# A mixture of experts on one core: experts ordered by token count on the chip, and narrow passes for the small ones

## The chip, the core and the metric

The kernel runs on one core of one Trainium2 chip. The metric is the device time of one execution in microseconds (us), as the median of several runs. A core has an engine for matrix products (TensorE, in the rows PE for its matmuls and PEld for its weight loads), VectorE (DVE), ScalarE (ACT), GpSimd (POOL) and SyncE (SP), which here mostly issues transfers, and 16 DMA engines that move data between the chip's memory (HBM) and the core's own.

## The reference

The program is a decoder of two layers on 256 tokens of 1,024 values. Each layer has a stage of three token mixers with a common projection, which this change leaves alone but for one small matmul, and then a mixture of 16 experts. The router picks, for every token, one of four groups of experts and in it two experts. The reference computes every expert on all tokens and weighs them with the gates, which are zero for the experts not chosen:

```python
gates = jnp.einsum('bske,bsk->bse', jax.nn.one_hot(top_idx, N_EXPERTS, dtype=jnp.float32), top_w).astype(h.dtype)
out = jnp.zeros_like(h)
for e in range(N_EXPERTS):
    a = jax.nn.silu(h @ w_gate[e]) * (h @ w_up[e])
    out = out + (gates[..., e:e + 1] * a) @ w_down[e]
```

`w_gate` and `w_up` of an expert are 1,024 x 512, `w_down` is 512 x 1,024, all float32: 6 MB an expert and 96 MB a layer (1 MB is 1,048,576 bytes here).

## The kernel before, in words

The function `moe()` (from line 833) computes one layer's experts. It needs no expert on all tokens: each expert gets 64 slots (`CAP`), and the tokens that chose it are put into them in the order of their number. The router (lines 880 to 930) leaves, for each token and expert, `rk`, the place of the token among that expert's tokens, counted from 1 and zero where the token did not choose it, and `gate`. `nf` (lines 938 to 940) is the number of 64-slot passes each expert needs.

**Gather.** `group()` (line 1130) compares `rk` with 1 to 64 for four experts at once, which gives a 0/1 matrix `Pm` of 256 tokens by 4 x 64 slots. `gather()` (line 966) multiplies the tokens' values by it on TensorE: for each of 8 blocks of 128 values four matmuls, for two halves of the tokens and for the values split into two fp32r parts `hi` and `lo` (line 974). The results `xg` hold the slots of four experts side by side in 256 columns. A group is gathered when the last expert of the group before has been started.

**One expert, a step of the loop at line 1150.** SP issues its loads: four `w1slot` transfers of 1 MB for gate and up (line 99, in a ring of 11 buffers that all stages share) and three `wd` transfers (two of 0.5 MB at line 1158, with 5 buffers, and one of 1 MB at line 1160, with 2 buffers). SP issues in program order; a transfer whose buffer is still being read holds up all transfers behind it. TensorE then does, mixed with each other by the table `CAB`:

- `up()` (line 1005): 16 matmuls in fp32, each of which the trace records as two, with the expert's 64 slots as the stationary matrix and 512 columns of weights moving. There are two column tiles of 64 (`j`): each holds one half of the expert's hidden values, its gate and up columns in one row of 512;
- `act()` (line 1013): Silu on ACT and the product on DVE, giving `a`; `turn()` (line 1019) transposes it with two matmuls against `ident` (`paT`), and DVE copies it out as `aT`;
- `down()` (line 1027): 8 matmuls `py` of 512 columns, again in two column tiles; ACT and DVE scale them with the gate and split them into `yy`;
- `scatter_tables()` (line 991): the one-hot matrix of the expert transposed (`ppg`, line 994) and its gate column (line 996), as `pT` and `gc`;
- `combine()` (line 1050): 8 matmuls that add the expert's rows to the tokens' places in four accumulators `mo` (line 1060). The last expert of a layer uses its other form, `flat`, with 16 matmuls of 64 rows (line 1055).

The turn, down and combine of an expert lie in the next expert's step (`pend`). `GROUPS = (1, 0, 2, 3)` makes experts 4 to 7 the first group of either layer.

**Overflow.** `extras()` (line 1063) works out, in the first step and on DVE, how many further passes of 64 slots are needed and for which experts. After the loads and the up pass of the step at position 8 (`OVE`), `overflow()` (line 1081) has TensorE, ACT, DVE and SP read that number and branch; for each further pass, `round_()` (line 1101) loads the expert's 6 MB again on SP by a register address (line 1092, four ring buffers `w1ovf`) and does gather, up, down and combine for up to 64 tokens. At most 7 rounds are built into the code, one inside another.

In `trunk()`, lines 243 to 246 write a constant `dup`, two halves of `ident` twice each, which one small matmul at line 516 uses in the mixers' stage.

## Time and profile before

| what | us |
|---|---|
| median of 3 runs | 933.82 (932.88 to 934.24) |
| the profiled execution, its own time | 933.14 |
| the span in its trace | 931.4 |

| engine | busy us in the span | share |
|---|---|---|
| TensorE, matmuls (PE) | 835.0 | 90% |
| VectorE (DVE) | 470.1 | 50% |
| ScalarE (ACT) | 292.0 | 31% |
| GpSimd (POOL) | 77.6 | 8% |

299.10 MB (10^6 bytes) are moved, at a mean of 321 GB/s; the mean granted clock of TensorE is 0.961 of full speed. The experts of layer 0 take the span from about 217 to 475 us, those of layer 1 from about 652 to 925 us. A row of the timeline gives the start in us from the span's start, the duration in us, the engine, the line, the operation, output and inputs by their names, the tile and shape, and how many instructions it stands for; brackets give an idle time before it and what ended it. An fp32 matmul is recorded as two. Matmuls that overlap in the pipeline or in different tiles each show their own time, so the pace is read from starts and not from durations.

### The profile page before, as it was taken

What the parts mean: (1) busy time and instruction counts of PE and PEld (TensorE: products, weight loads), DVE (VectorE), ACT (ScalarE), POOL (GpSimd) and SP (SyncE); (2) the same over time, 40 slices, a digit from 0 to 9 for tenths busy, and PEclk for the clock granted to TensorE, in tenths of its full rate; (3) what the DMA queues carried; (4) which work ended last, traced back from release to release, by engine and by line L of the source; (5) the groups of instructions that cost most, each with busy time, mean ns of one, the idle gap of its engine ahead of it and who ended that gap; (6) DMA issues with size and microseconds to landing.
All of it is one profiled execution on the core that took longest, in us unless ns stands there. A gap on an engine that the chain in (4) does not pass through costs nothing. (4 is left out here: it accounts for less than half of the span.)

```text
span 931.4 us, 12309 instructions
## 1 busy us (share of the span) xinstructions
PE 835.0 (90%) x4646; PEld 474.5 (51%) x4646; DVE 470.1 (50%) x1132; ACT 292.0 (31%) x676; POOL 77.6 (8%) x84
## 2 busy tenths in 40 slices
PE   4799989768999998999979989998999999799995
PEld 3677558744343343343358766786334344234332
DVE  7979989974232132222167998976222213122222
ACT  6255756331111020111155546754111112011110
POOL 2132001310000000000013220111000000000000
PEclk8899899978999999999999989998999999899998
DMA  8958688777999968999955694685889998399981
GB/s 362 419 193 336 274 353 283 274 316 301 370 417 373 395 255 334 420 417 419 419 201 175 246 404 174 238 310 217 301 328 413 376 405 336 141 421 417 418 349 46
DMA packets 47877, 299.10 MB, mean 321 GB/s; under 512 B 5568, under 2 KB 6336, under 8 KB 16320
## 3 DMA queue, kind: packets, MB, share of 16 engines
q1 hardware_dynamic: 46368, 296.05, 80.8%
q10 hardware_dynamic: 1440, 2.16, 0.8%
q8 instruction: 40, 0.66, 0.3%
q14 instruction: 29, 0.24, 0.1%
HBM read 297.13 MB, written 1.05 MB: 320 GB/s over the span
## 5 line engine op out<-in xcount | busy, mean ns | idle before, releaser
L1009 PE MATMUL pgu<-w1slot,xg 128*64 128x512 f32 x1024 | 273.3, 608 | 3.4 <-PEq L1102 3.4
L1009 PEld LDWEIGHTS pgu<-w1slot,xg 128*64 128x64 f32 x1024 | 71.9, 137 | 115.9 <-issue 107.4
L1043 ACT ACTIVATE yy<-py,gc 64x512 fp32r<-64x512 f32 x60 | 41.0, 683 | 227.8 <-PE py L1032 190.1
L1016 DVE TENSOR_TENSOR a<-a,pgu 128x256 f32<-128x256 f32 x33 | 13.9, 421 | 168.2 <-ACT a L1015 168.2
L189 DVE SCALAR_TENSOR_TENSOR adaslot<-adaslot,sb__90 128x1024 f32<-128x1024 f32 x72 | 94.7, 1325 | 0.0
L998 DVE CAST pgT<-ppg 128x256 fp32r<-128x256 f32 x33 | 14.0, 425 | 145.3 <-PE ppg L996 145.3
L344 PE MATMUL pz<-hhi,whl 128*128 128x256 f32 x256 | 73.1, 296 | 10.1 <-ACT hhi L415 10.1
L345 PE MATMUL pz<-hlo,whl 128*128 128x256 f32 x256 | 75.0, 296 | 0.8 <-DVE hlo L416 0.7
L346 PE MATMUL pz<-hhi,whl 128*128 128x256 f32 x256 | 74.3, 296 | 1.0 <-DVE whl L340 1.0
L1015 ACT ACTIVATE a<-pgu 128x256 f32<-128x256 f32 x33 | 12.7, 385 | 191.3 <-PE pgu L1009 191.3
L340 POOL TENSOR_TENSOR whl<-winslot,whl 128x512 fp32r<-128x512 f32 (+1 forms) x24 | 35.2, 1467 | 408.1 <-ACT whl L338 359.1
L1032 PE MATMUL py<-wd,aT 128*64 128x512 f32 x256 | 61.4, 592 | 0.0
L1044 DVE SCALAR_TENSOR_TENSOR yy<-py,gc,yy 64x512 fp32r<-64x512 f32 x60 | 45.0, 750 | 25.7 <-ACT yy L1043 24.7
L1060 PEld LDWEIGHTS mo<-pgT,yy 128*128 128x128 f32 x240 | 32.0, 188 | 49.5 <-DVE yy L1044 47.9
L344 PEld LDWEIGHTS pz<-hhi,whl 128*128 128x128 f32 x256 | 49.5, 198 | 14.2 <-ACT hhi L415 12.9
L345 PEld LDWEIGHTS pz<-hlo,whl 128*128 128x128 f32 x256 | 51.0, 199 | 2.4 <-DVE hlo L416 1.7
L346 PEld LDWEIGHTS pz<-hhi,whl 128*128 128x128 f32 x256 | 50.5, 198 | 2.1 <-DVE whl L340 1.4
L338 ACT CAST whl<-winslot 128x512 fp32r<-128x512 f32 (+1 forms) x72 | 40.3, 577 | 24.2 <-PE pz L346 23.6
L1060 PE MATMUL mo<-pgT,yy 128*128 128x256 f32 x240 | 44.3, 306 | 0.8 <-DVE yy L1044 0.8
L340 DVE TENSOR_TENSOR whl<-winslot,whl 128x512 fp32r<-128x512 f32 (+1 forms) x48 | 35.0, 733 | 10.1 <-ACT whl L338 10.1
L346 PE MATMUL pw<-yhi,whl 128*128 128x256 f32 x128 | 36.5, 291 | 3.5 <-DVE whl L340 3.5
L344 PE MATMUL pw<-yhi,whl 128*128 128x256 f32 x128 | 37.1, 292 | 1.1 <-DVE sge L711 0.7
(490 smaller groups left out, 1390.7 us busy)
## 6 DMA issues: line engine op xcount, KB each, us to landing
w1slot<-w_dram SPq DMA_DIRECT2D x128, 1024.0 KB, 12.2
adaslot<-adaw_dram SPq DMA_DIRECT2D x40, 1024.0 KB, 6.9
wd<-wd_dram SPq DMA_DIRECT2D x32, 1024.0 KB, 7.7
winslot<-win_dram SPq DMA_DIRECT2D x14, 1024.0 KB, 9.9
slot<-adaw_dram SPq DMA_DIRECT2D x8, 1024.0 KB, 18.9
woslot<-wout_dram SPq DMA_DIRECT2D x8, 1024.0 KB, 10.4
slot<-win_dram SPq DMA_DIRECT2D x6, 1024.0 KB, 18.2
cmpslot<-cmpw_dram SPq DMA_DIRECT2D x4, 1024.0 KB, 8.3
```

The lines of the kernel that those rows point to most:

```text
L189: V.scalar_tensor_tensor(wb, wb, 1.0, sb_, op0=OP.mult, op1=OP.mult, accum_out=mv_[:, b:b + 1])
L338: A.copy(hi, wv)
L340: (G if wc[0] % WP[fl[0]] == 0 else V).tensor_tensor(lo, wv, hi.bitcast(F32), op=OP.subtract)
L344: T.matmul(o, a[0], b[0], start=start, stop=False, skip_group_check=True)
L345: T.matmul(o, a[0], b[1], start=False, stop=False, skip_group_check=True)
L346: T.matmul(o, a[1], b[0], start=False, stop=stop, skip_group_check=True)
L998: V.tensor_copy(pT, pp_[:, :S])
L1009: lastu[0] = T.matmul(gu[64 * j:64 * j + 64, :], xg(c)[:, xs:xs + CAP], w1(c, j), start=c == 0, stop=c == 7, skip_group_check=True).ins
L1032: T.matmul(py[64 * hf:64 * hf + 64, :], aT[:, ib, 64 * j:64 * j + 64], wd(fc)[:, 512 * hf:512 * hf + 512], start=fc == 0, stop=fc == 3, sk ...
L1043: ya = A.activation(y[0:64, :], py[r_, :], AF.Copy, scale=gc[r_, :])
L1044: V.scalar_tensor_tensor(y[64:128, :], py[r_, :], gc[r_, :], y[0:64, :].bitcast(F32), op0=OP.mult, op1=OP.subtract)
L1060: T.matmul(mo[db // 2][:, S * (db % 2):S * (db % 2) + S], yy[db // 4][:, P * (db % 4):P * (db % 4) + P], pT, start=False, stop=False, skip ...
```

## The change

All of it lies in `moe()` but for the removal of `dup`. It does six things.

1. **A sort on the chip.** Experts 4 to 7 stay first and keep their 64 slots (`NST`, `ST0`). The other twelve are ordered by their token count, largest first: `sort()` builds a key of 16 times the count plus the expert's number (the four static ones get a key far below), compares all pairs, sums to a rank, and with one-hot products writes `rk`, `gate`, the count and the expert's number in the new order (`rkP`, `gP`, `inP`, `idI`). It runs on DVE, right behind the first group's gather. `extras()` works on the new order and is some instructions longer.
2. **Loads by address.** For positions 4 to 15 SP reads the expert's number from `idI` into a register and loads `w1` and `wd` from there (lines 1258 to 1268 of the changed kernel).
3. **Slots by position.** Positions 0 to 9 have 64 slots; position 4, the largest expert, has 32 more, in a pass of its own with the same weights (`"x"`); positions 10 to 15 have 32. The gathers of the four groups, `XGR`, are 256, 224, 224 and 160 columns wide.
4. **A pass of 32 slots.** `up_few()` uses four column tiles of 32 with 256 moving columns, 32 matmuls in place of 16 of 512; `act()` works on 128 columns of gate and 128 of up on all 128 partitions, and `turn()` is one transpose. `down_few()` has 16 matmuls of 256 columns in place of 8 of 512, and `combine_few()` 16 of 32 rows in four row tiles.
5. **Overflow.** `OVE` goes from 8 to 12, the rounds from 7 to 8. The rounds' weights go through one buffer of 0.5 MB, in twelve pieces, on POOL's queue in place of SP's; SP no longer branches, POOL does (`ENG3` in place of `ENG4`).
6. **Small ones.** `dup` is replaced by two matmuls against halves of `ident`, and the eight last additions into `xT` stand in another order.

The core of the diff:

```diff
+SW = 32
+NST = 4
+ST0 = 4
+HOT = 4
+NBIG = 10
+CAPS = [CAP] * HOT + [CAP + SW] + [CAP] * (NBIG - HOT - 1) + [SW] * (NE - NBIG)
+XGR = (((0, 0, CAP), (1, 64, CAP), (2, 128, CAP), (3, 192, CAP)),
+       ((4, 0, CAP), (5, 64, CAP), (6, 128, CAP), ("x", 192, SW)),
+       ((7, 0, CAP), (8, 64, CAP), (9, 128, CAP), (10, 192, SW)),
+       ((11, 0, SW), (12, 32, SW), (13, 64, SW), (14, 96, SW), (15, 128, SW)))
...
-ENG4 = (mybir.EngineType.PE, mybir.EngineType.Activation, mybir.EngineType.DVE, mybir.EngineType.SP)
-NOVF = 7
-OVE = 8
+ENG3 = (mybir.EngineType.PE, mybir.EngineType.Activation, mybir.EngineType.DVE, mybir.EngineType.Pool)
+NOVF = 8
+OVE = 12
...
+        def sort():
...
+            key = sm_([16], "nf")
+            V.scalar_tensor_tensor(key, idn[:, 1, :], 16.0, kc, op0=OP.mult, op1=OP.add)
...
+            V.tensor_tensor(cmp_, key.unsqueeze(1).to_broadcast([P, 16, 16]), key.unsqueeze(2).to_broadcast([P, 16, 16]), op=OP.is_ge)
+            rank = sm_([16], "gat")
+            V.tensor_reduce(rank, cmp_, axis=AX.X, op=OP.add)
...
+            for src, dst in ((idn, inP), (rk, rkP), (gate, gP)):
+                for r in range(2):
+                    tm = tl("k1", [nd, 16], "tmq")
+                    V.tensor_tensor(tm, oh, src[:, r, :].unsqueeze(1).to_broadcast([P, nd, 16]), op=OP.mult)
+                    V.tensor_reduce(dst[:, r, NST:], tm, axis=AX.X, op=OP.add)
...
+        def up_few(xg, xs, w1, gu=None, cs=range(8)):
+            gu = gu or bank("W", "pgu")
+            for c in cs:
+                for t in range(4):
+                    wv = w1(c, t // 2).rearrange("p (g k n) -> p g k n", g=2, k=2)[:, :, t % 2, :]
+                    lastu[0] = T.matmul(gu[SW * t:SW * t + SW, 0:256], xg(c)[:, xs:xs + SW], wv, start=c == 0, stop=c == 7,
+                             skip_group_check=True).ins
+            return gu
...
+        def down_few(aT, wd, pT, gc):
+            py = bank("W", "py")
+            for fc in range(4):
+                for q in range(4):
+                    T.matmul(py[SW * q:SW * q + SW, 0:256], aT[:, 0, SW * fc:SW * fc + SW], wd(fc)[:, 256 * q:256 * q + 256],
+                             start=fc == 0, stop=fc == 3, skip_group_check=True)
+            return flat_parts(py, gc, 256)
...
+        def combine_few(yy, pT):
+            for u in range(2):
+                for i in range(2):
+                    for q in range(4):
+                        r_ = slice(SW * q, SW * q + SW)
+                        T.matmul(mo[q][:, S * u:S * u + S], yy[i][r_, P * u:P * u + P], pT[r_, :], start=False, stop=False,
+                                 skip_group_check=True)
...
-            n = nc.values_load(ei[0:1, NOVF:NOVF + 1], engines=ENG4, min_val=0, max_val=NOVF)
...
-                    keep.append([g_["ring"].tile([P, 2048], F32, tag="slot", name="w1ovf") for _ in range(4)])
...
+            n = nc.values_load(ei[0:1, NOVF:NOVF + 1], engines=ENG3, min_val=0, max_val=NOVF)
...
+                er = nc.values_load(ei[0:1, r:r + 1], engines=ENG3[3:], min_val=0, max_val=NE - 1)
+                wt = tl("f4", [1024], "wov")
...
+                        G.dma_start(wt, src[:, c // 4, :, 1024 * (c % 4):1024 * (c % 4) + 1024].rearrange("o p n -> (o p) n"))
...
+                        er = nc.values_load(idI[0:1, e:e + 1], engines=(mybir.EngineType.SP,), min_val=0, max_val=NE - 1)
+                        s1 = I["w1"][l][bass.ds(er, 1)]
```

The order of the instructions on an engine, as a scheduler sets it, moves at three places. `xN` counts equal instructions in a row. The first is TensorE, layer 0, in the step of one of the last experts: `paT` is the turn, `py` the down pass, `ppg` the tables, `mo` the combine of the expert before. Before:

```order
L1022 MATMUL paT<-ident,a 128x128 x2
L1009 MATMUL pgu<-w1slot,xg 64x512 x4
L1032 MATMUL py<-wd__3788,aT 64x512 x2
L1032 MATMUL py<-wd__3790,aT 64x512 x2
L1032 MATMUL py<-wd_3792,aT 64x512 x4
L994 MATMUL ppg<-ident,Pd 128x128 x2
L996 MATMUL ppg<-lg,Pd 128x1 x2
L1009 MATMUL pgu<-w1slot,xg 64x512 x3
L1060 MATMUL mo_2115<-pgT,yy_3887 128x256 x2
```

With the change, at the same place:

```order
L1074 MATMUL paT<-ident,a 128x128
L1060 MATMUL pgu<-w1slot,xg 32x256 x8
L1109 MATMUL py<-wd__4520,aT 32x256 x4
L1109 MATMUL py<-wd__4522,aT 32x256 x4
L1109 MATMUL py<-wd_4524,aT 32x256 x8
L1036 MATMUL ppg<-ident,Pd 128x128 x2
L1038 MATMUL ppg<-gP,Pd 128x1 x2
L1060 MATMUL pgu<-w1slot,xg 32x256
L1131 MATMUL mo_2121<-pgT,yy_4669 128x256
L1131 MATMUL mo_2122<-pgT,yy_4669 128x256
```

The sequence is the same; up and down have twice the matmuls at half the columns, and the turn has one transpose.

The second is TensorE, layer 0, from the first expert's tables to the second expert's down pass; `cmx` holds the number of overflow rounds. Before:

```order
L994 MATMUL ppg<-ident,Pd 128x128 x2
L996 MATMUL ppg<-lg,Pd 128x1 x2
L1009 MATMUL pgu<-w1slot,xg 64x512 x16
L1022 MATMUL paT<-ident,a 128x128 x2
L1009 MATMUL pgu<-w1slot,xg 64x512 x4
L1032 MATMUL py<-wd__2183,aT 64x512 x2
```

With the change:

```order
L1038 MATMUL ppg<-lg,Pd 128x1 x2
L1051 MATMUL pgu<-w1slot,xg 64x512 x15
L1166 TENSOR_LOAD cmx
L1166 ISA x2
L1074 MATMUL paT<-ident,a 128x128 x2
L1051 MATMUL pgu<-w1slot,xg 64x512 x4
L1084 MATMUL py<-wd__2226,aT 64x512 x2
```

TensorE's load of the number of rounds has moved up from the step of position 8 to right behind the first up pass.

The third is SP, around the loads of late experts. Before, in layer 0, the overflow code stands in its queue behind the loads of position 8:

```order
L1158 DMA wd__2881<-wd_dram 128x1024
L1158 DMA wd__2883<-wd_dram 128x1024
L1160 DMA wd_2885<-wd_dram 128x2048
L1082 TENSOR_LOAD cmx
L1102 COMPARE_AND_BRANCH
L1086 TENSOR_LOAD cmx
L1086 ISA x2
L1092 ISA
L1092 DMA w1ovf<-w_dram 128x2048
```

With the change, in layer 1, behind the last loads that the mixers' stage and the first four experts need; the row of `idI` and the one behind it stand there twelve times in a row, for all twelve sorted experts, before the fifth expert's four `w1slot` loads:

```order
L1266 DMA wd__6924<-wd_dram 128x1024
L1266 DMA wd__6926<-wd_dram 128x1024
L107 DMA w1slot<-w_dram 128x2048 x2
L1266 DMA wd__6998<-wd_dram 128x1024
L1258 TENSOR_LOAD idI
L1258 ISA x2
```

No overflow load stands in SP's queue any more, and its loads from the fifth expert on stand behind the reads of `idI`.

## Rows read from the trace of the kernel before

**Rows 1.** The head of the profile page.

```profile
span 931.4 us, 12309 instructions
```

**Rows 2.** Busy time by stretch: stretch, length, PE, PEld, DVE, ACT, POOL, PEclk, DMA share, GB/s.

```profile
217.00:475.00 258.00, 239.77 (x1140) 98.36 (x1138) 62.23 (x157) 38.89 (x67) 1.28 (x1) 1.00 0.93 373
652.00:925.00 273.00, 256.79 (x1207) 104.18 (x1206) 66.55 (x173) 38.83 (x68) 0.00 (x0) 0.99 0.83 333
360.00:460.00 100.00, 93.49 (x438) 38.03 (x436) 23.70 (x58) 14.14 (x24) 0.00 (x0) 1.00 1.01 419
```

**Rows 3.** Timeline of TensorE, layer 0, the step at position 10.

```profile
370.88 0.44 PE L1022 MATMUL paT<-ident,a 128*128 128x128 f32 x2 [0.93 <-DVE a L1016]
371.25 1.94 PE L1009 MATMUL pgu<-w1slot,xg 128*64 128x512 f32 x8
373.01 1.03 PE L1032 MATMUL py<-wd__3714,aT 128*64 128x512 f32 x4
...
376.55 0.44 PE L994 MATMUL ppg<-ident,Pd 128*128 128x128 f32 x2
...
386.04 0.44 PE L1022 MATMUL paT<-ident,a 128*128 128x128 f32 x2 [0.93 <-DVE a L1016]
```

**Rows 4.** Timeline of TensorE, layer 0, the gather and the two steps around it.

```profile
400.42 0.28 PE L974 MATMUL pgx<-Pm,lo 128*128 128x256 f32 x1
400.54 0.28 PE L974 MATMUL pgx<-Pm,hi 128*128 128x256 f32 x1
...
404.14 0.38 PE L1022 MATMUL paT<-ident,a 128*128 128x128 f32 x2
...
419.88 0.44 PE L1022 MATMUL paT<-ident,a 128*128 128x128 f32 x2 [0.93 <-DVE a L1016]
```

**Rows 5.** Timeline of SP, layer 0: the loads around the expert at position 11.

```profile
362.47 7.86 SPq L99 DMA_DIRECT2D w1slot<-w_dram  x4
372.50 0.33 SPq L1158 DMA_DIRECT2D wd__3862<-wd_dram  x1
```

**Rows 6.** Waits of SP's queue: line, what ended them, us in all, count, longest.

```profile
SPq L1158 <- PE py L1032: 152.9, 24, 10.7
```

**Rows 7.** Timeline of TensorE, layer 1, around the step that holds the overflow round.

```profile
770.61 0.38 PE L1022 MATMUL paT<-ident,a 128*128 128x128 f32 x2
...
812.40 0.69 PE L1022 MATMUL paT<-ident,a 128*128 128x128 f32 x2
```

**Rows 8.** Groups of instructions by shape: count, busy us and mean ns, idle before and releaser.

```profile
L531 PE MATMUL ph<-cmpslot,E 128*32 128x128 f32 x128 | 3.9, 274 | 0.0
...
L1055 PE MATMUL mo<-pgT,yy 64*128 64x256 f32 x48 | 4.4, 303 | 3.4 <-ACT yy L1036 1.7 <-ACTq L1102 0.8 <-DVE yy L1037 0.6
```

**Rows 9.** Timeline of DVE, layer 0, the end of the first up pass.

```profile
226.12 0.42 DVE L1016 TENSOR_TENSOR a<-a,pgu 128x256 f32<-128x256 f32 x1 [5.47 <-ACT a L1015]
```

**Rows 10.** Timeline of SP, layer 1: early w1 loads, and the overflow code.

```profile
653.95 5.48 SPq L99 DMA_DIRECT2D w1slot<-w_dram  x4
...
758.29 0.33 SPq L1160 DMA_DIRECT2D wd<-wd_dram  x1
759.86 1.99 SPq L1092 DMA_DIRECT2D w1ovf<-w_dram  x4
```

**Rows 11.** Timeline of TensorE: layer 0's end, layer 1's position 10, layer 1's end.

```profile
466.79 0.44 PE L1022 MATMUL paT<-ident,a 128*128 128x128 f32 x2 [0.93 <-DMA winslot<-win_dram]
...
473.03 0.97 PE L1055 MATMUL mo<-pgT,yy 64*128 64x256 f32 x12 [0.28 <-DVE yy L1037]
...
827.12 0.44 PE L1022 MATMUL paT<-ident,a 128*128 128x128 f32 x2
...
923.70 0.97 PE L1055 MATMUL mo<-pgT,yy 64*128 64x256 f32 x12 [0.28 <-DVE yy L1037]
```

**Rows 12.** Busy time by stretch, TensorE alone: stretch, length, PE, PEclk, DMA share, GB/s.

```profile
205.00:210.00 5.00, 0.00 (x0) 0.50 0.99 401
215.00:220.00 5.00, 5.00 (x35) 0.87 1.01 421
```

More of the change, by code (lines that the diff above doesn't have):

```diff
@@ L966, in gather @@
         def gather(Pm, n, xg_):
[L967 removed]
+            per = 2
             for c0 in range(0, 8, per):
@@ L1034, in down @@
             if flat:
[L1035 to L1038 removed]
+                return flat_parts(py, gc, 512)
             yy = []
@@ L1104, in round_ @@
                         reuse.append({})
-                    w1, wd = load(r)
+                    w1, wd = weights(r)
                     oh = sml([16], "st")
@@ L1149, in moe @@
+        rkP, gP, inP, idI, rkx = sort()
         pend = None
[L1150 to L1188 removed]
@@ L1189, in moe, with tables_ @@
-        combine(down(turn(pend[0]), *pend[1:], LFL), pend[2], LFL)
-        for m in (0, 4, 1, 5, 2, 6, 3, 7) if LFL else range(8):
+        for g4, members in enumerate(XGR):
+            order = sorted(members, key=lambda m: HOT + 0.5 if m[0] == "x" else m[0])
+            for k, (p, xo_, w) in enumerate(order):
+                e = HOT if p == "x" else p
+                few = w == SW
+                if p != "x":
+                    if e < NST:
+                        s1, sd = [I["w1"][l, ST0 + e, i] for i in range(2)], I["wd"][l, ST0 + e]
+                    else:
+                        er = nc.values_load(idI[0:1, e:e + 1], engines=(mybir.EngineType.SP,), min_val=0, max_val=NE - 1)
+                        s1 = I["w1"][l][bass.ds(er, 1)]
+                        s1 = [s1[:, i].rearrange("o p n -> (o p) n") for i in range(2)]
+                        sd = I["wd"][l][bass.ds(er, 1)].rearrange("o p n -> (o p) n")
+                    wa = [t.rearrange("p (c j n) -> p c j n", c=2, j=2) for i in range(2) for t in slots(s1[i], "w1slot")]
+                    wb = []
+                    for i in range(2):
+                        wb.append(tl("wh", [1024], "wd_"))
+                        Y.dma_start(wb[i], sd[:, 1024 * i:1024 * i + 1024])
+                    w2_ = tl("c6", [2, 1024], "wd2")
+                    Y.dma_start(w2_, sd[:, 2048:4096].rearrange("p (f n) -> p f n", f=2))
+                    wb += [w2_[:, 0], w2_[:, 1]]
+                w1 = lambda c, j, wa=wa: wa[c // 2][:, c % 2, j, :]
+                wd = lambda fc, wb=wb: wb[fc]
+                up_ = up_few if few else up
+                CA, CB = next(x[:2] for x in CAB[l] if e < x[2]) if k else CAB0
+                def tables_():
+                    if p == "x":
+                        return scatter_tables(one_hot(rkx, w), gP, HOT)
+                    if e < NST:
+                        return scatter_tables(one_hot(rk[:, :, ST0 + e], w), gate, ST0 + e)
+                    return scatter_tables(one_hot(rkP[:, :, e], w), gP, e)
+                gu = up_(xgs, xo_, w1, None, range(CA)) if CA else None
+                if pend:
+                    aT = turn(pend[0])
+                gu = up_(xgs, xo_, w1, gu, range(CA, CB))
+                if pend:
+                    (combine_few if pend[4] else combine)((down_few if pend[4] else down)(aT, *pend[1:4]), pend[2])
+                pT, gc = tables_()
+                gu = up_(xgs, xo_, w1, gu, range(CB, 8))
+                pend = (act(gu, 128 if few else 256), wd, pT, gc, few)
+                if p != "x":
+                    with fence_(rk_, F2):
+                        g_["fill"](FILL[l][6][e])
+                if e == 0:
+                    ovf = extras()
+                if k == len(order) - 1 and g4 < 3:
+                    xgs = group(g4 + 1, rank_of)
+                if e == OVE:
+                    overflow(*ovf)
+                if e == RES:
+                    last[2] = lastu[0]
@@ L1191, in moe @@
+        combine_few(down_few(turn(pend[0]), *pend[1:4]), pend[2])
+        for m in (0, 2, 4, 6, 1, 3, 5, 7):
             b, u = m // 2, m % 2
```

186 lines of the change are left out of this document (95 added, 91 removed).

## The prediction

> **What bounds the kernel now.** I read the page's head first, for the span of 931.4 us [rows 1], then the busy time by stretch, to see which stages the change touches and what is full there. The mixture of experts runs from 217 to 475 us in layer 0 and from 652 to 925 in layer 1, 531 us together; TensorE is busy about 240 of 258 and 257 of 273 us there, and the DMA engines move 373 and 333 GB/s [rows 2]. In the later part of layer 0, 360 to 460 us, the transfers run at 419 GB/s with a DMA share of 1.01, while TensorE is also 93% busy [rows 2]: the two limits lie close together, and a gain on TensorE alone is soon stopped by the other. One expert is 6 MB (of 1,048,576 bytes), at 419 GB/s 15.0 us.
>
> The timeline of TensorE gives its own price. A step runs from one `paT` to the next: 370.88 to 386.04, 15.16 us [rows 3]. Its up matmuls are 32 records, the first 8 of them 1.76 us (371.25 to 373.01), so 0.22 us each and 7.0 in all; `py` with the tables' start at 376.55 takes 3.54 us; 4.6 us are left for the turn, the wait for `a` (0.93), tables, combine and changes of tiling [rows 3]. The step at a group's end is longer by the gather: 386.04 to 404.14 is 18.10 us, and the next one, to 419.88, 15.74, so a gather costs some 3.5 us [rows 3, 4]. The `pgx` matmuls in it start 0.12 us apart [rows 4].
>
> How far ahead the loads are comes from SP's own timeline: the four `w1slot` loads of expert 11 are issued from 362.47 to 370.3, just before step 10 starts, and only then come its `wd` loads [rows 5]. SP stands in line behind a `wd` buffer until the down matmuls of two experts earlier have read it: 24 waits, 152.9 us [rows 6]. So when TensorE gets faster, the loads are about one expert and a half ahead, not more.
>
> **The change part by part.** The reference's router, with the reference's inputs, gives no expert over 64 tokens in layer 0 and one with 65 in layer 1, which is the one overflow round in this trace. Sorted without experts 4 to 7, the counts are 51 44 42 39 39 34, then 31 30 29 28 18 17; and 65 55 52 49 47 24, then 23 22 18 15 15 15. They fit 96, five times 64 and six times 32, so no round should run.
>
> *Overflow round in layer 1, removed.* The step that holds it lasts from 770.61 to 812.40, 41.8 us; the same place without it (404.14 to 419.88) takes 15.74 [rows 4, 7]: **-26.0 us**. The untaken branch stays.
>
> *A 32-slot pass in place of a 64-slot pass, f.* Up is 64 records of 256 columns in four column tiles. If four run side by side, 0.055 us each by rows 3 (half the columns, twice the tiles: 0.22/4), 3.5 us. `ph` already runs in four such tiles: 128 records of 128 columns in 3.9 us, 0.0305 each [rows 8], 0.061 for 256 columns, 3.9 us. I take 3.7, and 1.85 for the 32 records of down. Combine becomes 16 matmuls of 32 rows; the same form with 64 rows, used three times in the trace, takes 4.4 us for 48 records [rows 8], 1.5 us for 16, and I count no gain or loss against today's 8. So f = 3.7 + 1.85 + 4.6 = **10.2 us**; lower bound 9.4 (3.5, 1.75, and half the combine), upper bound the full 15.2, were four tiles no faster than two. The Trainium skill, *TensorE: Matmul & The Clock Gate*, "Measured speedup vs the span model", reports 2.38 times for three column tiles and 3.07 for four row tiles, so less than the number of tiles. By that f would be an estimated 11.4, and the time some 10 us above my sum; the `ph` row stands nearer to full overlap.
>
> *The extra pass of the largest expert* (ranks 65 to 96) lies among the steps that TensorE paces: **+10.2 per layer**.
>
> *The sort and the register loads.* Some 25 DVE instructions on 16 to 256 columns and a longer `extras` fall into the gather and the first up pass. One of 256 columns takes 0.42 us, and DVE idles 5.47 us ahead of it [rows 9]; at most 10 us of new work, I think 7, meet that room and some in the gather. TensorE now loads the round count behind the first up pass and waits for the end of `extras`: I take **+1 per layer**, between 0 and 3. On SP two register loads, a branch and register arithmetic fit between 758.62 (758.29 + 0.33) and 759.86 [rows 10], under 0.6 us each; in layer 1 all twelve stand in a row ahead of the fifth expert's loads, some 7 us. There the transfers have room (all 11 ring slots are filled, and SP's next w1 loads go out only at 653.95, when the first up pass has begun to free them [rows 10]), so nothing is on the path; without that room they would cost these 7 us once. Loads of the overflow code off SP cost or give nothing while no round runs. The gathers of groups 1 and 2 are 224 columns wide, of group 3 160: -0.5 per layer if time follows columns.
>
> *The last six experts.* Step 10 starts at 370.88 in layer 0, and the stage ends at 474.0 (473.03 + 0.97): 103.1 us. In layer 1 it is 827.12 to 924.7, 97.6 us [rows 11]. Now TensorE alone would need 6f, 1.7 for expert 9's full down pass, 3.2 for the gather and 5.4 for the last turn, down and combine (today 466.8 to 474.0 [rows 11], less 1.8): 71.5 us. The transfers need more: at the start of step 10 expert 11's w1 is issued and its tail `wd` is not, so 26 to 30 MB are to come, at 2.50 us per MB 65 to 75 us, and 3 to 5 us of down and combine follow the last byte: 68 to 80. I take **75 us** for both layers; what is late next is the loads, about 15 us an expert. The Trainium skill, *DMA: Bandwidth & Descriptors*, "Where 436 GB/s comes from", says that the HBM side, about 358 GB/s per core, binds such loads; by that this part would take an estimated 12 us more per layer, but the trace differs (419 for 100 us [rows 2]), and the measurement decides.
>
> *Clock.* While it waits for weights TensorE has gaps. With no matmul from 205 to 210 us its granted clock is 0.50 (1.2 GHz), and from 215 to 220, with matmuls throughout, still 0.87 [rows 12]. I put 2 us per layer for a start of the following stage at the low level (0 to 6).
>
> *Sum.* Layer 0: 10.2 + 1 - 0.5 + 75 - 103.1 = -17.4. Layer 1: -26.0 + 10.2 + 1 - 0.5 + 75 - 97.6 = -37.9. With 4 for the clock -51.3, so a span of 880.1, and with the 1.7 us around the span of the profiled execution (933.14 against 931.4) **882 us**. That execution is 0.7 us under the median of 933.82 of the runs shown, which doesn't matter here.
>
> **The rivals.**
> *Narrow gathers are dear (to 916).* Every fp32r matmul of the trace moves 256, 280 or 512 columns; the new gathers move 224 and 160. Should such a matmul fall back to the fp32 rate (0.44 us per record of 512 columns when alone, two records: 1.72 ns per column, from rows 3), 224 columns take 0.385 in place of 0.105 us and a gather of 32 gains 9.0 us. Two of them are paced by TensorE, the third lies mostly beside the transfers: +17 per layer, 882 + 34 = 916. Against it: nothing in the trace speaks for such a step; for it: no row excludes it.
>
> *Four tiles are no faster than two (slower, to 942).* Then f = 15.3, TensorE paces everything, and the sum is 14f - 205.1 (7f + 10.8 per layer, less 103.1, 97.6 and 26): +9.1, 940.5 and 1.7, 942. The point from which the change loses is f = 14.6. The place is the up and down loops of the small experts. Against it: the `ph` row, at 0.0305 us a record, would then be 0.05 or more.
>
> *The rounds are not gone (923, or 964 with two).* Then the change does not do what it says. A round costs 26.0 us today with its weights ahead; now it loads twelve 0.5 MB pieces through one buffer, each behind the readers of the one before, so the 15.0 us of transfer come on top: 41, or 923 us with one round and 964 with one in each layer. Against it: the counts.
>
> *The transfers are slower in the last part (to 899).* At the stage's mean of 373 GB/s in place of 419 [rows 2] the 70 us of bytes become 79, +9 per layer. The mean has SP's waits in it, and 100 us at 419 speak against it.
>
> *Better than forecast (to 864).* If w1 of expert 11 has landed at step 10's start and the clock holds, 68 us and no 4: 14 + 4 less.
>
> **How the numbers follow.** About 0.2% (1.9 us) is what a measurement of this kernel can tell from no change. Forecast with its own range 0.62 (864 to 895: a small pass 0.7 us longer in 14 places, 3 us in place of 1 at both register loads); narrow gathers 0.24; slower transfers 0.04; four tiles no faster 0.06; rounds still run 0.02; something that just eats the gain 0.02. Faster: 0.62 + 0.24 + 0.04 = 0.90, same 0.02, slower 0.08. The range for 8 in 10 goes from the lower end of the forecast to the narrow gathers: 864 to 916.
>
> **What would show it.** Right: no `w1ovf` or `wov` load; w1 loads that land evenly about 15 us an expert over the last six, TensorE waiting for `w1slot` there; a small pass of 9 to 11 us; stage ends near 457 and 870 us (the second by the first stage's 17 us earlier start). Wrong: `pgx` matmuls of 224 columns more than 0.2 us apart; `pgu` records of 256 columns about 0.11 us apart; TensorE waiting on the register load for more than 3 us; gaps between transfers in the last six experts.

## The result, and the profile after

| | before | the change |
|---|---|---|
| median, first sitting | 934.03 us (n = 4) | 909.76 us (897.57 to 911.79, n = 4) |
| ratio, with its 95% interval | | 0.9651 [0.9564, 0.9739] |
| profiled execution, its span | 933.14, 931.4 us | 911.16, 909.5 us |

The change is faster by 3.5%. The ratio is formed from the undisturbed executions alone, of the change 897.57 and 908.36 us and not the profiled one, and so differs from that of the medians. The forecast was 882 us, with a range of 864 to 916.

The head of the profile page of the changed kernel, and its line on TensorE:

```profile
span 909.5 us, 14341 instructions
PE 794.5 (87%) x5460; PEld 476.1 (52%) x5460; DVE 461.0 (51%) x1175; ACT 278.8 (31%) x663; POOL 75.8 (8%) x89
```

TensorE is busy 40 us less than before. The busy time by stretch of the changed kernel (columns as in [rows 2], the number after POOL being PEclk): the experts of layer 0, of layer 1, and the last six of layer 0.

```profile
218.00:468.00 250.00, 223.91 (x1601) 102.10 (x1601) 63.49 (x199) 33.58 (x63) 0.00 (x0) 0.95 0.92 367
652.00:902.00 250.00, 225.63 (x1601) 103.77 (x1601) 63.66 (x197) 32.52 (x61) 0.00 (x0) 0.94 0.85 339
390.00:468.00 78.00, 64.69 (x772) 33.56 (x772) 15.21 (x53) 8.87 (x20) 0.00 (x0) 0.89 1.02 418
```

Against [rows 2] two things are new. In the last 78 us of layer 0 the transfers run at a share of 1.02 and TensorE is busy in only 65 of them. And the granted clock, which was 1.00 and 0.99 in the experts' stages, is 0.95 and 0.94.

Where the time went is best seen by stages, each bounded by rows of TensorE's timeline: the first router matmul (`prank`) of a layer, the first turn (`paT`), the last combine (`mo`). The same table holds the profiles of the experiments below; every number is the difference of two such rows.

| profile of | first `prank` at | layer 0: to first turn | then to end | to `prank` of layer 1 | to first turn | then to end | rest | span |
|---|---|---|---|---|---|---|---|---|
| before | 211.0 | 15.6 | 247.4 | 170.2 | 17.3 | 263.1 | 6.7 | 931.4 |
| the change | 216.8 | 21.0 | 230.3 | 182.5 | 24.7 | 226.2 | 8.0 | 909.5 |
| a_again | 209.7 | 21.4 | 230.1 | 175.9 | 22.4 | 226.1 | 8.1 | 893.7 |
| a_sort_late | 210.5 | 16.6 | 229.4 | 173.4 | 16.9 | 226.0 | 8.0 | 880.8 |
| a_no_branch | 214.8 | 21.0 | 229.6 | 175.7 | 22.5 | 226.5 | 7.7 | 897.9 |
| a_light_tail | 213.4 | 20.1 | 221.5 | 172.6 | 22.6 | 214.1 | 8.2 | 872.5 |
| b_before_noround | 209.0 | 15.9 | 247.0 | 175.5 | 16.8 | 237.4 | 6.6 | 908.2 |
| b_inter | 211.2 | 21.3 | 221.3 | 173.7 | 22.7 | 218.0 | 8.0 | 876.1 |
| b_inter_late | 216.4 | 16.5 | 223.0 | 172.6 | 16.9 | 216.7 | 8.0 | 870.2 |
| b_late_fill | 210.4 | 16.5 | 228.9 | 170.4 | 16.9 | 226.1 | 8.0 | 877.2 |
| c_no_x | 209.7 | 21.4 | 221.2 | 170.1 | 22.7 | 218.6 | 7.8 | 871.4 |
| c_wide | 211.1 | 21.1 | 246.2 | 176.8 | 24.8 | 237.5 | 7.4 | 924.8 |
| c_inter_late_fill | 209.6 | 16.9 | 226.2 | 169.6 | 16.9 | 224.8 | 8.0 | 872.1 |

From its first turn on, a layer became shorter by 17.1 and 36.9 us, where the forecast's terms gave 18.4 and 38.9. The other columns go the other way: up to the first turn (+5.4, +7.4), the mixers' stage of layer 1 (+12.3), that of layer 0, which is in the first column (+5.8), and the rest (+1.3).

**The first expert waits for the sort.** TensorE's timeline of the changed kernel, layer 0:

```profile
226.30 0.30 PE L1036 MATMUL ppg<-ident,Pd 128*128 128x128 f32 x1 [2.99 <-DVE Pd L1027]
...
228.53 8.32 PE L1051 MATMUL pgu<-w1slot,xg 128*64 128x512 f32 x30
237.78 0.44 PE L1074 MATMUL paT<-ident,a 128*128 128x128 f32 x2 [0.93 <-DVE a L1067]
```

VectorE's timeline, in the same place (the rank, the last sorted gates, the first expert's one-hot matrix):

```profile
219.29 0.41 DVE L1004 TENSOR_REDUCE gat<-cmq 128x16 f32<-128x256 f32 x1
...
225.28 0.61 DVE L1014 TENSOR_REDUCE gP<-tmq 128x12 f32<-128x192 f32 x2
225.80 0.16 DVE L1020 TENSOR_SCALAR rkx<-rkP 128x2 f32<-128x2 f32 x1
225.87 0.48 DVE L1027 TENSOR_SCALAR Pd<-iot,rk 128x128 f32<-128x128 f32 x2
```

The sort's instructions stand in VectorE's queue among the copies (`xg`) that empty the gather's results, and ahead of `Pd`, which the first expert's tables need. TensorE waits 2.99 us for it, and its first up pass then takes 8.32 us for 30 records, where the kernel before took 7.09 for 32; part of it is at the lower clock (granted 0.76 from 225 to 230 us, 1.00 before).

**A small pass.** TensorE's timeline of the changed kernel, layer 0, from one turn to the next among the last six:

```profile
438.19 0.33 PE L1074 MATMUL paT<-ident,a 128*128 128x128 f32 x1 [0.71 <-DVE a L1067]
438.45 1.07 PE L1060 MATMUL pgu<-w1slot,xg 128*32 128x256 f32 x16
439.33 0.61 PE L1109 MATMUL py<-wd__4520,aT 128*32 128x256 f32 x8
...
443.88 2.36 PE L1060 MATMUL pgu<-w1slot,xg 128*32 128x256 f32 x38
446.94 0.33 PE L1074 MATMUL paT<-ident,a 128*128 128x128 f32 x1 [0.71 <-DVE a L1067]
```

It takes 8.75 us where [rows 3] had 15.16. The 16 records from 438.45 to 439.33 start 0.055 us apart, a quarter of the 0.22 of [rows 3]: half the columns each, in twice as many tiles. Four tiles ran fully side by side.

**The end of the layer.** The same timeline, the overflow branch and the last expert:

```profile
426.77 0.45 PE L1074 MATMUL paT<-ident,a 128*128 128x128 f32 x1 [4.78 <-PEq L1188]
...
454.19 1.07 PE L1060 MATMUL pgu<-w1slot,xg 128*32 128x256 f32 x16 [1.00 <-DMA w1slot<-w_dram]
456.68 1.94 PE L1060 MATMUL pgu<-w1slot,xg 128*32 128x256 f32 x16 [1.42 <-DMA w1slot<-w_dram]
459.17 1.93 PE L1060 MATMUL pgu<-w1slot,xg 128*32 128x256 f32 x16 [0.56 <-DMA w1slot<-w_dram]
...
466.97 1.15 PE L1131 MATMUL mo<-pgT,yy 32*128 32x256 f32 x16 [0.64 <-ACT yy L1101]
```

and the chain of waits there (start, us, what):

```profile
418.18 18.52 DMA w1slot<-w_dram
436.71 17.43 DMA w1slot<-w_dram
454.21 14.12 DMA winslot<-win_dram
```

The last up pass runs at the pace of its four 1 MB transfers, 2.5 us apart. The chain goes through transfers from 418 us on. TensorE's 4.78 us of waiting at the branch (`PEq` is its sequencer) are not in it.

### The profile page after: what moved, and what is told of

It reads as the page before. It is cut to its first block, busy times and chain, and to the rows that moved or that the text cites. A ratio compares the mean times of both kernels' runs of the same rounds, so it can differ in the third digit from the quotient of the medians.

```text
span 909.5 us, 14341 instructions
## 1 busy us (share of the span) xinstructions
PE 794.5 (87%) x5460; PEld 476.1 (52%) x5460; DVE 461.0 (51%) x1175; ACT 278.8 (31%) x663; POOL 75.8 (8%) x89
## 4 chain that ended last, share of the span: by engine, by line
PE 58%; DVE 22%; DMA 14%; ACT 3%; issue 2%; ACTq 0%; SPq 0%; DVEq 0%
PE pgu L1051 18%; DMA w1slot<-w_dram 11%; PE py L1084 8%; DVE adaslot L197 6%; PE pgx L985 3%; DVE whl L350 3%; PE mo L1123 3%; PE pgu L1060 3%; PE sc L644 2%; DVE slot L197 2%; PE pz L355 2%; PE pz L354 2%; DMA winslot<-win_dram 2%; PE pz L356 2%; PE pm L321 1%
## 5 line engine op out<-in xcount | busy, mean ns | idle before, releaser
L1051 PE MATMUL pgu<-w1slot,xg 128*64 128x512 f32 x640 | 172.8, 614 | 0.0
L1067 DVE TENSOR_TENSOR a<-a,pgu 128x256 f32<-128x256 f32 (+1 forms) x34 | 12.5, 366 | 168.6 <-ACT a L1066 163.0
L197 DVE SCALAR_TENSOR_TENSOR adaslot<-adaslot,sb__90 128x1024 f32<-128x1024 f32 x72 | 92.2, 1292 | 0.0
L1060 PE MATMUL pgu<-w1slot,xg 128*32 128x256 f32 x896 | 72.7, 416 | 13.6 <-DMA w1slot<-w_dram 8.4
L1051 PEld LDWEIGHTS pgu<-w1slot,xg 128*64 128x64 f32 x640 | 45.7, 139 | 73.5 <-issue 68.2
L1092 ACT ACTIVATE yy<-py,gc 64x512 fp32r<-64x512 f32 x40 | 27.3, 683 | 145.3 <-PE py L1084 119.7
L1066 ACT ACTIVATE a<-pgu 128x256 f32<-128x256 f32 (+1 forms) x34 | 11.5, 340 | 193.6 <-PE pgu L1051 127.8
L348 ACT CAST whl<-winslot 128x512 fp32r<-128x512 f32 (+1 forms) x72 | 40.5, 578 | 26.1 <-PE pz L356 24.2
L1060 PEld LDWEIGHTS pgu<-w1slot,xg 128*32 128x32 f32 x896 | 28.1, 115 | 38.5 <-issue 13.6
L1084 PE MATMUL py<-wd,aT 128*64 128x512 f32 x160 | 38.7, 592 | 0.0
L1093 DVE SCALAR_TENSOR_TENSOR yy<-py,gc,yy 64x512 fp32r<-64x512 f32 x40 | 30.0, 750 | 15.7 <-ACT yy L1092 15.0
## 6 DMA issues: line engine op xcount, KB each, us to landing
woslot<-wout_dram SPq DMA_DIRECT2D x8, 1024.0 KB, 11.4
```

Of the source, the lines that this page charges most:

```text
L197: V.scalar_tensor_tensor(wb, wb, 1.0, sb_, op0=OP.mult, op1=OP.mult, accum_out=mv_[:, b:b + 1])
L348: A.copy(hi, wv)
L1051: lastu[0] = T.matmul(gu[64 * j:64 * j + 64, :], xg(c)[:, xs:xs + CAP], w1(c, j), start=c == 0, stop=c == 7, skip_group_check=True).ins
L1060: lastu[0] = T.matmul(gu[SW * t:SW * t + SW, 0:256], xg(c)[:, xs:xs + SW], wv, start=c == 0, stop=c == 7, skip_group_check=True).ins
L1084: T.matmul(py[64 * hf:64 * hf + 64, :], aT[:, ib, 64 * j:64 * j + 64], wd(fc)[:, 512 * hf:512 * hf + 512], start=fc == 0, stop=fc == 3, sk ...
L1092: ya = A.activation(y[0:64, :], py[r_, :], AF.Copy, scale=gc[r_, :])
```

## The experiments

The times of a sitting are compared with the kernel before on the same chip: 931.97 us for the runs a, 933.76 for b and 934.97 for c (11 executions each). Each letter is another chip, so where runs of different letters are set against each other, the stages of the table decide and not the medians.

**a_again: the change once more.**

> The changed kernel, unaltered, to see how its two mixers' stages vary. Their code is the same as before, yet in the first profile the one of layer 1 (end of layer 0's last combine to the router's prank matmuls) took 182.5 us against 170.2, with TensorE at the granted clock 0.50 from 550 to 570 us. Theory A, chance of the clock: the times spread over 12 us or more between executions, as 897.6 and 911.8 did, and a profile's mixers' stages vary by as much. Rival, the change makes these stages slower each time: all times lie at 908 to 912 us and the stage takes 180 to 185 us again.

899.13 us (895.28 to 904.91, n = 6), ratio 0.9671 [0.9621, 0.9721]; the kernel before spread from 928.13 to 943.75 in this sitting. From the first turn on its layers take 230.1 and 226.1 us, as in the first profile to 0.2 us. Its mixers' stage of layer 1 takes 175.9 against 182.5, and the first `prank` comes at 209.7 against 216.8. The rival falls: no time lies at 908 to 912 us, and 13.7 of the 15.8 us between the two profiles lie in stages that the change leaves alone. Theory A holds for the stages; the times spread over 9.6 us, less than the 12 it gave. A weaker rival is left, that the change makes these stages a little slower on the whole; it is taken up below. The granted clock of TensorE shows what differs. Busy time of TensorE by stretch (length, busy, PEclk, DMA share, GB/s), in the kernel before:

```profile
540.00:550.00 10.00, 7.13 (x99) 1.00 1.01 421
550.00:560.00 10.00, 9.66 (x50) 0.66 1.01 419
560.00:570.00 10.00, 10.00 (x53) 1.00 0.20 82
```

and in the changed kernel, first profile:

```profile
540.00:550.00 10.00, 6.69 (x71) 0.92 1.01 423
550.00:560.00 10.00, 10.00 (x41) 0.50 0.98 407
560.00:570.00 10.00, 10.00 (x30) 0.50 0.04 15
570.00:580.00 10.00, 10.00 (x41) 0.71 0.10 12
```

In both TensorE has just stood idle for 3 us (3.21 and 3.13, for VectorE's `hid`) and then works without a gap. Before, it is back at 2.4 GHz within 10 us; here it is granted 1.2 GHz (0.50) for 20 us and more. In a_again it is back at the same place of the program after about 8 us, and then falls to 0.50 once more, from 550 to 562 us, with TensorE busy throughout. No run tells why the low level lasts longer in one execution than in another.

**a_sort_late: the sort behind the first expert's tables.**

```diff
-        rkP, gP, inP, idI, rkx = sort()
...
                 pT, gc = tables_()
+                if e == 0:
+                    rkP, gP, inP, idI, rkx = sort()
```

> The sort is called behind the first expert's tables in place of ahead of them. Theory A, the sort on VectorE holds up the first expert: the waits of ppg for Pd (2.99 and 3.84 us in the first profile) go, TensorE's gap ahead of its first up pass closes, and the time falls by 7 us, up to 13 us if the first up pass also keeps a higher clock (8.32 + 1.07 and 11.79 us of up pass against 7.09 and 9.65 before). Rival, the wait only moves: sort and extras, some 9 us on VectorE, now end behind the first up pass, where TensorE loads the round count, and the time falls by less than 3 us.

890.25 us (882.39 to 897.62, n = 6), 8.9 below a_again. TensorE's timeline of this kernel, layer 0:

```profile
217.09 0.38 PE L1036 MATMUL ppg<-ident,Pd 128*128 128x128 f32 x2
217.31 0.51 PE L1038 MATMUL ppg<-lg,Pd 128*128 128x1 f32 x4
217.75 7.09 PE L1051 MATMUL pgu<-w1slot,xg 128*64 128x512 f32 x32
227.05 0.44 PE L1074 MATMUL paT<-ident,a 128*128 128x128 f32 x2 [2.22 <-DVE a L1067]
```

The wait for `Pd` is gone, and the first up pass is at its full pace again (7.09 us, as in the kernel before). The stretch up to the first turn falls from 21.4 to 16.6 and from 22.4 to 16.9 us, 10.3 in all. About 1.3 us of the wait moves: VectorE, busy with the sort and `extras`, lets TensorE wait 2.22 us for `a` in place of 0.93.

**a_no_branch: no overflow code.** (No expert of these inputs needs a round, so nothing of the sum is left out.)

```diff
-                if e == OVE:
-                    overflow(*ovf)
```

> The overflow code is left out: no round count is read, no branch, no round for an expert with more tokens than slots. In the first profile TensorE waits 4.78 and 5.11 us at this branch. Theory A, the transfers set the end of either layer: the wait lies beside them and the time falls by 0 to 3 us. Rival, TensorE sets it: the time falls by 8 to 10 us, more if the clock (0.78 in the 10 us with the wait) holds.

899.36 us (891.42 to 907.86, n = 6): no difference to a_again, and layers of 229.6 and 226.5 us. The step that held the branch in layer 0 takes 8.76 us in place of 12.83, but later steps wait nearly as much longer for weights. The 4.78 and 5.11 us at the branch lie beside the transfers.

**a_light_tail: the last two experts of a layer load nothing.**

```diff
-                if p != "x":
+                if p != "x" and e < 14:
                     if e < NST:
```

> The last two experts of a layer load no weights and use those of position 13 (12 MB a layer less moved; the sum is that of other weights). Theory A, the transfers set the end: without these 30 us of transfer TensorE alone paces the last six experts, 6 small passes of 8.9 us, 1.7 and 3.2 for the rest of expert 9 and the gather, 5.4 at the end and 4.8 for the branch, 68 us in place of the 78 from 389.96 to 468.1 us: 10 us a layer, 20 in all, a few more from the clock. Rival, TensorE and its clock set the end: the time falls by less than 6 us.

874.91 us (872.45 to 881.53, n = 6), 24.2 below a_again; the layers are shorter by 8.6 and 12.0 us. Busy time of TensorE by stretch in this kernel, near layer 0's end:

```profile
430.00:440.00 10.00, 9.29 (x157) 1.00 0.95 392
440.00:450.00 10.00, 9.18 (x139) 1.00 0.18 48
```

The transfers stop at about 440 us and TensorE goes on at its own pace and full clock. The last six experts take 69.3 and 67.6 us, where theory A had 68. So it is the transfers that hold the last six experts, as the forecast had it.

**b_before_noround: the kernel before without its overflow code** (one token of expert 3 in layer 1 is left out).

```diff
-            if e == OVE:
-                overflow(*ovf)
```

> The kernel before, without its overflow code: no branch, no round (in layer 1 one token of expert 3 is left out). Theory A, the step with the round is on TensorE's path: 26.0 us fewer by the prediction's term, 26 to 31 with the waits at the branch. Rival, the loads that run during the round give part of it back later: 10 to 20 us.

910.89 us (902.21 to 912.88, n = 6), 22.9 below the kernel before. By the profiles layer 1 falls from 263.1 to 237.4, 25.7 us: the term of 26.0 stands, and nothing of it is given back within the layer. Its mixers' stage, in code that is wholly that of before, takes 175.5 us against 170.2; this too moves by 5 us without any change.

**b_inter: small experts between large ones.**

```diff
-       ((4, 0, CAP), (5, 64, CAP), (6, 128, CAP), ("x", 192, SW)),
-       ((7, 0, CAP), (8, 64, CAP), (9, 128, CAP), (10, 192, SW)),
-       ((11, 0, SW), (12, 32, SW), (13, 64, SW), (14, 96, SW), (15, 128, SW)))
+       ((10, 0, SW), (11, 32, SW), (4, 64, CAP), ("x", 128, SW), (5, 160, CAP)),
+       ((12, 0, SW), (6, 32, CAP), (13, 96, SW), (7, 128, CAP)),
+       ((8, 0, CAP), (14, 64, SW), (9, 96, CAP), (15, 160, SW)))
...
-            order = sorted(members, key=lambda m: HOT + 0.5 if m[0] == "x" else m[0])
+            order = members
```

> The changed kernel with its twelve sorted experts worked in another order, small ones between large ones: 10 11 4 x 5, 12 6 13 7, 8 14 9 15 (gathers 224, 192 and 192 wide). From 230 to 390 us of layer 0 the transfers stood still for some 15 us in all, 7 of them beside the x pass, and from 390 us on they never stood still. Theory A, the bytes set a layer's length and only idle transfers can be won back: 8 to 14 us a layer, 16 to 28 in all. Rival, small passes ahead of large ones wait for weights and the clock falls in those waits: no gain, or up to 10 us slower.

878.07 us (873.41 to 881.45, n = 6), ratio 0.9391 [0.9339, 0.9443]; the layers are shorter by 8.8 and 8.1 us than in a_again. Busy time of TensorE by stretch, at the x pass of the changed kernel:

```profile
300.00:310.00 10.00, 9.07 (x74) 1.00 0.73 280
310.00:320.00 10.00, 9.29 (x101) 1.00 0.29 93
```

and of this kernel in the same stretch, whose x pass comes behind two small experts and a large one, from 314 us on:

```profile
300.00:310.00 10.00, 9.29 (x87) 1.00 1.01 406
310.00:320.00 10.00, 9.07 (x60) 1.00 1.02 417
```

The x pass uses weights that are already there; it frees nothing, SP stands behind full buffers, and the transfers pause. With two small experts ahead of it the transfers do not pause there: in layer 0 their share is 1.02 over the whole of 290 to 450 us. Theory A holds, at its lower end. The gain is that of leaving the x pass out (8.9 and 7.5 us in c_no_x), and no run moved the x pass alone or spread the small experts alone, so what each of the two is worth is not shown.

**b_inter_late: that order and the late sort.**

> The other order of experts and the late sort together. Theory A, the two are independent: the gain of the order and the 8.9 us of the late sort add up, 25 to 37 us below the changed kernel. Rival, a first expert that starts 5 us earlier only finds the transfers that much later: less than 3 us below the other order alone.

872.19 us (870.56 to 874.83, n = 6), ratio 0.9333 [0.9285, 0.9381]: 26.9 us below a_again and 5.9 below the order alone. By the stages of the experts (both layers, with the stretches up to the first turn) the order alone is 16.7 us shorter than a_again, the late sort alone 11.1 and the two together 26.9: the gains add up to within 1 us, and this version is faster than both kernels.

**b_late_fill and c_inter_late_fill: zeros to hold the clock.** Added to a_sort_late and to b_inter_late:

```diff
+                if p == 15:
+                    for c2 in range(CB, 8, 2):
+                        zfill(4)
+                        gu = up_(xgs, xo_, w1, gu, range(c2, c2 + 2))
+                    zfill(4)
...
+        def zfill(n):
+            for i in range(n):
+                T.matmul(mo[i % 4], zb, zb.unsqueeze(1).to_broadcast([P, 4, P]), start=False, stop=False, skip_group_check=True)
```

> The late sort, and 20 matmuls with zeros into mo among the last expert's up pass, where TensorE waits for the pieces of w1 (nothing is added to the sum). Theory A, the low clock at a layer's end (0.67 from 450 to 470 us) costs time in the last pass and in the start of the next stage: 2 to 6 us fewer than with the late sort alone. Rival, the transfers set this end and the clock's cost there is small: within 2 us, or slower by the matmuls added.

> The other order of experts, the late sort and the 20 matmuls with zeros among the last expert's up pass. Theory A, the higher clock at a layer's end carries over into the next stage, as it did with the late sort alone (mixers' stage of layer 1 in 170.4 us against 173.4): 868 to 870 us, 2 to 4 below the 872.2 without the zeros. Rival, that was chance: 872 within 1.5 us.

With the late sort alone they gave 884.63 us (877.83 to 893.04), ratio 0.9451 [0.9390, 0.9512] against a_sort_late's 0.9580 [0.9527, 0.9633], but the layers are the same to 0.5 us: 228.9 and 226.1 against 229.4 and 226.0. The 5.6 us below a_sort_late lie in the mixers' stages or between the sittings. With the other order they gave 881.50 us (873.67 to 892.29), 9.3 more than b_inter_late, which neither theory had. Here the layers are longer, 226.2 and 224.8 us against 223.0 and 216.7. Busy time of TensorE by stretch at the end of layer 1, b_inter_late:

```profile
845.00:855.00 10.00, 7.88 (x61) 1.00 0.64 262
855.00:865.00 10.00, 5.41 (x89) 1.00 0.01 2
```

and c_inter_late_fill, with two rows of its timeline:

```profile
845.00:855.00 10.00, 9.65 (x75) 1.00 0.10 41
855.00:865.00 10.00, 7.25 (x90) 1.00 0.00 0
```

```profile
814.64 1.93 PE L1060 MATMUL pgu<-w1slot,xg 128*32 128x256 f32 x16 [6.55 <-issue]
...
850.77 1.25 PE L1247 MATMUL mo<-zb 128*128 128x512 bf16 x5
```

With the other order the transfers are done at about 851 and 846 us, and the layer ends at 862.2 and 864.1: TensorE sets the end there, and the zeros (`zb`) lie on its path. The step that holds them takes 16.16 and 16.17 us in the two layers, against 12.37 without: 3.8 us a layer. The other 4.3 of layer 1's 8.1 us arise ahead of the zeros, where TensorE stands for 6.55 us; the profile names no cause for that, and it is left open. Beside transfers the zeros cost nothing. That the clock they hold is what made b_late_fill's time lower was not shown: its mixers' stage of 170.4 us lies in the range that the unchanged code has by itself.

**c_no_x: no extra pass for the largest expert** (its tokens from the 65th on are left out; no overflow code).

```diff
-       ((4, 0, CAP), (5, 64, CAP), (6, 128, CAP), ("x", 192, SW)),
+       ((4, 0, CAP), (5, 64, CAP), (6, 128, CAP)),
```

> The changed kernel without the extra pass of the largest expert (its tokens from the 65th on are left out) and without the overflow code. Theory A, the pass lies where TensorE paces, as the prediction's term of 10.2 us a layer has it: the transfers no longer stand still beside it and a layer ends 7 to 9.5 us earlier, 14 to 19 in all. Rival, the bytes set a layer's length whatever TensorE does in its middle: less than 5 us in all.

885.11 us (873.19 to 888.05, n = 6), ratio 0.9492 [0.9441, 0.9543], 14 below a_again; the layers are 8.9 and 7.5 us shorter. The overflow code that is left out too moved nothing in a_no_branch. The pass is on the path, as the forecast had it.

**c_wide: 64 slots for all** (no extra pass, no overflow code, one token left out).

```diff
+XGR = tuple(tuple((4 * g + i, 64 * i, CAP) for i in range(4)) for g in range(4))
...
-        combine_few(down_few(turn(pend[0]), *pend[1:4]), pend[2])
+        combine(down(turn(pend[0]), *pend[1:4], True), pend[2], True)
```

> The sort and the loads by register address stay, but every expert has 64 slots, with no extra pass and no overflow code (the 65th token of one expert in layer 1 is left out). Theory A, the sort by itself saves nothing and the narrow passes carry the gain: layers as long as in the kernel before without its overflow code (247.0 and 237.4 us from the first turn to the end), and 5 us a layer for the wait on the sort, so 10 us above that kernel's 910.9, 921 us. Rival, loads by address or the other order of experts move the time as well: further than 4 us from it.

926.62 us (916.90 to 932.27, n = 4). The layers, 246.2 and 237.5 us from the first turn, are those of b_before_noround to 0.8 us, and the stretch up to the first turn is 5.2 and 8.0 us longer than there. Sort and loads by address save nothing by themselves, as theory A has it; the narrow passes, less the x pass, take 16.1 and 11.4 us off a layer (246.2 and 237.5 to 230.1 and 226.1). The whole time is 5.6 us above the number expected, further than the 4 us that were set for the rival; of this the first turn of layer 1 has 3, and the layers none, so the rest lies in the mixers' stages.

## Why the forecast was right, and where it was off

**Right: direction, range, and what bounds what.** 909.76 and 899.13 us lie in 864 to 916. That is in part luck: all ten executions of the changed kernel (895.28 to 911.79 us) lie above 895, where the forecast's own range ended, and inside the stated one only because it had been stretched to 916 for narrow gathers, which turned out not to be dear. The rival of rounds that still run fell with the first profile: no overflow load stands in it.

| step of the forecast | forecast, us | measured, us | from |
|---|---|---|---|
| overflow round | -26.0 | -25.7 | b_before_noround |
| small pass f | 10.2 (9.4 to 15.2) | 8.75 | timeline of after |
| x pass, a layer | +10.2 | +8.9, +7.5 | c_no_x |
| last six experts, a layer | 75 | 78.1, 79.7 | 389.96 to 468.12, 821.81 to 901.52 |
| sort and register load, a layer | +1 (0 to 3) | +5.4 to +7.4 | stages; 4.8 and 5.5 back in a_sort_late |
| narrow gathers, a layer | -0.5 | -0.5 | steps with a gather of 224 columns |
| clock, both layers | +4 | -2 to +18 | mixers' stages |

**A small pass** undercut even the lower bound, since the up pass reached full overlap and the 4.6 us of other work shrank too. It brought nothing more: the last six experts are paced by the transfers, and their part came out 3 to 5 us longer. Against that the x pass came out 1.3 and 2.7 us shorter, so the errors cancel in part, which is luck too. The estimate of 11.4 us a pass, drawn from the ratios of the Trainium skill, *TensorE: Matmul & The Clock Gate*, "Measured speedup vs the span model", for three column tiles and four row tiles, does not agree with this trace's 8.75 for four column tiles.

**Transfers in the last part.** They ran at 418 GB/s over 78 us, so the rival with the stage's mean of 373 fell. By the Trainium skill, *DMA: Bandwidth & Descriptors*, "Where 436 GB/s comes from", some 358 GB/s would bind such loads; the trace differs, and the measurement decides.

**Narrow gathers** were the forecast's largest rival. TensorE's timeline of the changed kernel, 224 columns and then 160:

```profile
340.08 0.27 PE L985 MATMUL pgx<-Pm,lo 128*128 128x224 f32 x1
340.19 0.27 PE L985 MATMUL pgx<-Pm,hi 128*128 128x224 f32 x1
...
402.93 0.28 PE L985 MATMUL pgx<-Pm,hi 128*128 128x160 f32 x1
403.05 0.28 PE L985 MATMUL pgx<-Pm,lo 128*128 128x160 f32 x1
```

The matmuls start 0.11 to 0.12 us apart at either width, so they are not dear. Nor do they save nothing: over a gather of 32 the matmuls start 0.111 us apart at 224 columns, where those of 256 do at 0.120 (two of them stand in [rows 4]), and the gather from its first start to its last takes 3.56 us in place of 3.81. The step that holds one shows it, from turn to turn, before and with the change:

```profile
256.92 0.44 PE L1022 MATMUL paT<-ident,a 128*128 128x128 f32 x2 [0.93 <-DVE a L1016]
275.01 0.38 PE L1022 MATMUL paT<-ident,a 128*128 128x128 f32 x2
```

```profile
268.11 0.44 PE L1074 MATMUL paT<-ident,a 128*128 128x128 f32 x2 [0.93 <-DVE a L1067]
285.94 0.38 PE L1074 MATMUL paT<-ident,a 128*128 128x128 f32 x2
```

18.09 us become 17.83; c_wide, whose gathers are 256 wide, has 18.09 too. Two such gathers a layer give the forecast's -0.5. Its reason, time that follows columns, holds only in part: at 192 (b_inter) and 160 columns the matmuls start 0.111 to 0.112 us apart, no closer than at 224.

**The step that failed is "the sort and the register loads".** It set the sort's 7 us against VectorE's idle time, 5.47 us ahead of `a` [rows 9]. That room lies behind the first expert's `Pd`. What counted was VectorE's queue ahead of `Pd`, which the forecast did not look at, and there the sort stands between two things that TensorE waits for. With the sort behind the tables (a_sort_late) the stretch up to the first turn is 1.0 us longer and 0.4 shorter than before: the +1 fits that order, and not the one it was given for. SP, by contrast, waits for the sort without harm, as the forecast's "nothing is on the path" has it (waits of SP's queue in the changed kernel: line, what ended them, us, count, longest; and its timeline behind that wait):

```profile
SPq L1258 <- DVE tmq L1013: 19.5, 1, 19.5
```

```profile
667.35 5.87 SPq L107 DMA_DIRECT2D w1slot<-w_dram  x4
```

These loads, the last one of the third expert and the first three of the fourth, and not the fifth's as the text ahead of the prediction has it, go out 3.7 us after the first up pass began (663.63), against 2.0 before (653.95 [rows 10], the pass from 651.97). In a_sort_late they go out 2.0 us after it again (639.16 and 637.18), and the layer behind the first turn is as long as in a_again, 226.0 against 226.1 us: the delay had cost nothing.

**The clock.** The forecast put 4 us for it. Over the profiles with the unchanged mixers' code of layer 1 the stage takes 169.6 to 182.5 us, and the first `prank` comes at 209.0 to 216.8. The profile of before, with 170.2 and 211.0, lay near the fast end of the first. Against it the first profile lost 18.1 us there and a_again 4.4 us (5.7 less 1.3). No execution of the changed kernel came near the forecast's 882; a_sort_late's profiled one, with the sort's wait gone, took 882.39. An estimate for the middle execution of a sitting: if all but the two mixers' stages takes what the profiles of before and of a_again show (550.2 and 508.1 us), the medians 931.97 and 899.13, less the 1.7 around the span, leave 380.1 and 389.3 us for them, some 9 us more with the change. Whether that is chance or comes of the change no run shows; the stage up to the first `prank` stands ahead of the changed code of `moe()` and still moved by 7.1 us between two profiles of the same kernel. The 1.9 us that the forecast took for what a measurement can tell were far too few: the kernel before spread over 15.6 us in one sitting.

By stages the span of a_again's profiled execution, the fastest of the six, differs from that of before by -1.3 + 5.8 - 17.3 + 5.7 + 5.1 - 37.0 + 1.4 = -37.6 us; the forecast had -51.3. Of the 13.7 between them, 8.9 are the sort (10.9 for 2), 3.0 the layers behind the first turn (-54.3 for -57.3), and some 2 the clock and the program's end.

**What stays open** is why the low clock lasts 20 us in one execution and less than 10 in another after the same idle time, whether the zeros held it, and whether the change itself makes the mixers' stages slower.

## What to carry to other kernels

When work is put into an engine's idle time, look at what stands behind it in that engine's queue and who waits for that; the size of the gap says nothing if the gap lies after the need. Where compute and transfers are close together, the order of pieces counts: here it was worth 17 us to put small experts ahead of the pass that reuses loaded weights and between large ones, in place of at the end, where the loads cannot keep up; which of the two did it was not separated. Before a small term is charged to a change, see how far the unchanged stages move between two profiles of the same kernel.

## What the runs showed that was not expected

- A branch on TensorE that is not taken, past eight nested rounds of code, cost 4.78 and 5.11 us of waiting; the 1.55 of the branch not taken in layer 0 before, with seven rounds, had not hinted at it. It was hidden here by transfers alone.
- fp32r matmuls in a row start 0.120 us apart at 256 moving columns and 0.111 to 0.112 at 224, 192 and 160: below 224 fewer columns gave no shorter step.
- Four column tiles of 32 with 256 moving columns reached a full fourfold overlap, 0.055 us a record, within a stretch of 16.
